# Rows of w_down gated with g2 beside the up projection and kept in DRAM, in a one-core diffusion block

## The chip, the core and the metric

The kernel runs on one core of one Trainium2 chip. The metric is the device time of one execution in microseconds (us). Three runs of the kernel before gave 1491.38, 1489.22 and 1489.94 us; the median is 1489.94 us. A core has a TensorE (PE, with its weight loads shown apart as PEld), a VectorE (DVE), a ScalarE (ACT), a GpSimd (POOL) and a SyncE (SP). Here SP issues every DMA, and each engine works through its own instructions in the order in which they were built.

## What is computed

One block of a diffusion transformer on 1024 tokens of width 1024: adaLN modulation, neighbourhood attention, output projection, and then a gated feed-forward part of width 2816 with a convolution over the tokens. The part that matters here is the last line:

```
def conv_ffn(h, w_up, conv_w, conv_b, w_down):
    a, g = jnp.split(h @ w_up, 2, axis=-1)
    return (a * jax.nn.gelu(dwconv_centred(g, conv_w, conv_b), approximate=False)) @ w_down

x = x + g2 * conv_ffn(modulate(rms_norm(x, p['norm2']), sh2, sc2), *p['ffn'])
```

`g2` is one row of 1024 numbers, the same for every token. Multiplying the result by `g2` is the same as multiplying every row of `w_down` by `g2` first, and this is what the kernel does, in both forms.

## The kernel before, in words

All matrix products are done with operands that are split into a rounded high part and a rest, so that each product is three matmuls (high x high, high x rest, rest x high). The high part is a copy on ACT, the rest a subtraction on DVE or POOL. Both projections of the feed-forward part use a Winograd form: seven products of half-size blocks in place of eight.

**Up projection** (L736 to L835). The 2816 columns come as 22 chunks of 128, taken in 11 blocks `i` of two chunks. A block has two parts, `part` 1 (the gate g) and `part` 0 (the value a), and each part has seven products `op`, in the order of `WORD`. That makes 154 steps; a step is 12 matmuls of 128x512. For each step `prep_up` (L678) makes the weight operand `u`: ACT copies the high part (L687), POOL subtracts the rest (L688). The operands live in 8 slots (tags `rh` and `rl`), so a new one can be made once PE has used an old one. DVE combines the seven products: `raw_up` (L673 to L675) and L686 form sums of weights, `put` (L757) adds PSUM banks and multiplies a by the gate, `conv` (L780) applies the token convolution, `finish` (L799) forms the sums for the down projection. SP stores them to `act_dram`.

**Down projection** (L837 to L931). The 11 blocks are taken in groups of 2, 3, 3 and 3, with seven products each. `load_raw` (L853) loads the two 128x1024 pieces of `w_down` of a block into tiles `dr` and multiplies them by `g2b`, the row g2 laid out on all 128 partitions: the piece `m` = 0 on POOL, the piece `m` = 1 on DVE. `prep_b` (L874) forms the Winograd sums of the pieces in place (L887 to L893) and splits them into `db` (L895 on ACT, L896 on DVE or POOL). `prep_a` (L865) loads the stored activations into `da` and splits them (L870 on ACT, L871 on DVE or POOL). `down_mm` (L899) multiplies, and DVE adds each bank onto the residual `acc` (L914).

What sets the order: the code is written as one stream, and a scheduler places each instruction on its engine's queue ahead of the run, earlier than written where it finds the engine free. The queues are then fixed. An instruction that waits holds everything behind it on its engine. The gate row `g2b` (L834) takes the slot of the first weight tile of the up projection, so it is there from the first few blocks on.

The lines that matter for the change:

```
SP.dma_start(out=r, in_=w_down[fc * P:(fc + 1) * P, :])
(DVE if m in DG else POOL).tensor_tensor(r, r, g2b, ALU.mult)
```

Of the kernel before, what the change touches and what calls it, by code (L numbers as in the profile page):

```python
# [10 lines left out]
F32 = mybir.dt.float32  # L11
F32R = mybir.dt.float32r
AF = mybir.ActivationFunctionType
ALU = mybir.AluOpType
# [4 lines left out]
P = 128  # L19
D = 1024  # L20
# [10 lines left out]
NF = DFF // P  # L31
# [5 lines left out]
HALF = 512  # L37
# [13 lines left out]
NA = ()  # L51
WD, SQD = range(8), ()
LAG = 1
DG = (1,)
HP_ = (3, 5, 6)
RL = 6
WORD = (1, 2, 5, 6, 7, 3, 4)
DORD = (2, 1, 5, 6, 3, 7, 4)

# [2 lines left out]
def block_kernel(ctx, tc, x, ctxt, cc, w_mod, b_col, b_row, n1, n2, w_qkv, gains, rpb_t, mask_i, mask_r, w_o,  # L62
                 w_up, conv_w, conv_b, w_down, comb, out):
    nc = tc.nc
    PE, ACT, DVE, POOL, SP = nc.tensor, nc.scalar, nc.vector, nc.gpsimd, nc.sync

    def pool(name, bufs=1, space=None, side=None):
        kw = {}
        if space is not None:
            kw["space"] = space  # L70
        if side is not None:
            kw["side"] = side
        if space is not DRAM:
            kw["reuse_waits"] = "tile"
        return tc.tile_pool(name=name, bufs=bufs, **kw)
# [8 lines left out]
    dram = ctx.enter_context(pool("dram", space=DRAM))  # L84
# [22 lines left out]
    o_dram = dram.tile([NPAIR, P, SEQ], F32, name="o_dram")  # L107
    g_dram = dram.tile([2, D], F32, name="g_dram")
    x1_dram = dram.tile([NB, P, D], F32, name="x1_dram")
    act_dram = dram.tile([NF // 2, P, 7, HALF], F32, name="act_dram")  # L110

    big = ctx.enter_context(pool("big", side="right"))
# [2 lines left out]
    def slot(tag, name, dt=F32R, shape=(P, D)):  # L115
        return big.tile(list(shape), dt, tag=tag, bufs=SLOTS[tag], name=name)
# [39 lines left out]
        DVE.tensor_scalar(ss, ss, 1.0 / D, EPS, ALU.mult, ALU.add)  # L156
        POOL.tensor_tensor(ss, ss, mhalf[:, 0:1], ALU.pow)

    # adaLN of the attention branch, normalised and modulated tokens, transposed and split
    att = ExitStack()  # L160
    sa = att.enter_context(pool("sa"))

# [106 lines left out]
            if si == 3:  # L269
                DVE.tensor_tensor(b1, pc[:, 1], bcol[:, 0:8].unsqueeze(2).broadcast_to([P, KC, 2]), ALU.add)  # L270

    # attention, with the projections of the next pair of heads in between
    sb = att.enter_context(pool("att"))
    mi = sb.tile([P, 3 * P], F32, name="mi")
    SP.dma_start(out=mi, in_=mask_i)
# [179 lines left out]
        DVE.tensor_tensor(res[a:b], po[a:b], tmp[a:b], ALU.add)  # L455
        SP.dma_start(out=o_dram[p, a:b, u * 2 * P:(u + 1) * 2 * P], in_=res[a:b])

    # adaLN of the rest, a little at a time
    def mod_gen():
        order = [2, 3, 4, 5]  # L460
        for sgi in order:
# [27 lines left out]
                        DVE.scalar_tensor_tensor(dst, dst, 1.0, n2c[:, nk * hf:nk * (hf + 1)], ALU.add, ALU.mult)  # L489
                yield  # L490

    # output projection: its first half runs beside the attention of the last heads
    xpool = ctx.enter_context(ExitStack())
    x1, wo, g1b, xsb = {}, [], [], []
    HP = NPAIR // 2
# [106 lines left out]
    filler(10 ** 6)  # L602
    att.close()

    # rest of the output projection, second norm, operands of the Winograd form (seven products of halves
    # in place of eight) of the up projection: A is w_up^T in 2 x 2 blocks, B the tokens in 2 x 2 blocks
    ff = ctx.enter_context(ExitStack())
    usb = ff.enter_context(pool("ffn"))
    BT = {}
    btags = ["bA"] * 12 + ["bB"] * 10 + ["wa"] * 6  # L610
    for i, op in enumerate(WORD):
        for j in range(4):
            tag = btags[4 * i + j]
# [3 lines left out]
            else:  # L617
                BT[op, hl, kk] = usb.tile([P, 2, HALF], F32R, tag=tag, bufs=12 if tag == "bA" else 10,
                                          name=f"b{op}{hl}{kk}")
# [26 lines left out]
            ACT.activation(h, r, AF.Copy)  # L646
            (POOL if op in HP_ else DVE).tensor_tensor(l, r, f(h), ALU.subtract)

    # up projection, gate with the token convolution; the gated rows and their sums go out for the down projection
    NP2 = NF // 2  # L650
    lo_, hi_ = slice(0, HALF), slice(HALF, SEQ)
    uraw, uop = {}, {}
    parts = [(i, part) for i in range(NP2) for part in (1, 0)]
    useq = [(0, 1, 1), (0, 1, 2), (0, 0, 1), (0, 0, 2)] + [(0, part, op) for part in (1, 0) for op in WORD[2:]]
    useq += [(i, part, op) for i, part in parts[2:] for op in WORD]
    cnt = [0]
# [21 lines left out]
    def prep_up(i, part, op):  # L678
        if (i, part) == (0, 1) and op in (1, 2):
            s = xslot(f"u{i}_{part}_{op}", F32R)  # L680
        else:
            s = slot(("rh", "rl")[cnt[0] % 2], f"u{i}_{part}_{op}", shape=(P, 2, HALF))
            cnt[0] += 1
        r = uraw[i, part]
        if op == 3:
            DVE.tensor_tensor(r[3], r[2], r[6], ALU.subtract)  # L686
        ACT.activation(s[:, 0], r[op], AF.Copy)  # L687
        POOL.tensor_tensor(s[:, 1], r[op], f(s[:, 0]), ALU.subtract)  # L688
        uop[i, part, op] = s
        if op == 4 and parts.index((i, part)) + 2 < len(parts):  # L690
            raw_up(*parts[parts.index((i, part)) + 2])
# [51 lines left out]
    def up_part(i, part, res):  # L743
# [23 lines left out]

        for op in WORD:
            bank = {1: x, 6: x, 2: z, 5: y, 3: y, 7: w, 4: w}[op]
# [10 lines left out]
    def conv(fc, g, y):  # L780
        ACT.activation(y, g, AF.Identity, bias=cb[:, fc:fc + 1], scale=cw[:, fc, 1:2])  # L781
        y8, g8 = (a.rearrange("p (m j) -> p m j", j=8) for a in (y, g))
        w0, w2 = cw[:, fc, 0:1], cw[:, fc, 2:3]
        R = ROWS

        def tap(o, i, w):
            DVE.scalar_tensor_tensor(o, i, w, o, ALU.mult, ALU.add)  # L787

        tap(y8[:, :, 1:], g8[:, :, :7], w0)
        tap(y8[:, R:, 0:1], g8[:, :-R, 7:8], w0)  # L790
        tap(y8[:, 1:R, 0:1], g8[:, (NB - 1) * R:NB * R - 1, 7:8], w0)
        tap(y8[:, :, :7], g8[:, :, 1:], w2)
        tap(y8[:, :-R, 7:8], g8[:, R:, 0:1], w2)
        tap(y8[:, (NB - 1) * R:NB * R - 1, 7:8], g8[:, 1:R, 0:1], w2)
        ACT.activation(y, y, AF.Gelu)
# [3 lines left out]
    def finish(i, y):  # L799
# [8 lines left out]
        SP.dma_start(out=act_dram[i, :, 3:5, :], in_=sa_)  # L808
        SP.dma_start(out=act_dram[i, :, 5:7, :], in_=sb_)

    sw = ps.tile([P, SEQ], F32, tag="s", bufs=1, name="sw")
    late_p1 = usb.tile([P, HALF], F32, name="late_p1")
    nprep, gens, g, y, late = 2, {}, {}, {}, []
    for k, (i, part, op) in enumerate(useq):
        while nprep < min(k + 1 + UA, len(useq)):
            prep_up(*useq[nprep])
            nprep += 1
        if (i, part) not in gens:
            if part:
                g[i] = [slot("wx", f"g{i}_{m}", F32) for m in range(2)]  # L820
                y[i] = [slot("t4", f"y{i}_{m}", F32) for m in range(2)]
            gens[i, part] = up_part(i, part, g[i] if part else y[i])
        next(gens[i, part])
        if op == WORD[-1]:
            if part:
                for m in range(2):
                    conv(2 * i + m, g[i][m], y[i][m])
                for o, p in late:
                    DVE.tensor_tensor(o, p, o, ALU.mult)
                late.clear()  # L830
            else:
                finish(i, y[i])
                if i == 0:
                    g2b = slot("gb", "g2b", F32)  # L834
                    SP.dma_start(out=g2b, in_=g_dram[1:2, :].broadcast_to([P, D]))  # L835

    # down projection, also in seven products; rows of w_down scaled by the gate g2  # L837
    xt = ps.tile([P, 2, HALF], F32, tag="s", bufs=1, name="dx")
    tr = [ps.tile([P, HALF], F32, tag="tr", bufs=3, name=f"dtr{j}") for j in range(3)]
    pq = [ps.tile([P, HALF], F32, tag="pq", bufs=2, name=f"dpq{j}") for j in range(2)]  # L840
# [12 lines left out]
    def load_raw(c):  # L853
        for m in range(2):
            if rt[0] % 14 < 8:
                r = xsb[0].tile([P, D], F32, tag="x1", bufs=NB, name=f"dr{c}_{m}")
            else:
                r = slot("wa", f"dr{c}_{m}", F32)
            rt[0] += 1
            fc = 2 * c + m  # L860
            SP.dma_start(out=r, in_=w_down[fc * P:(fc + 1) * P, :])
            (DVE if m in DG else POOL).tensor_tensor(r, r, g2b, ALU.mult)
            raws[c, m] = r

    def prep_a(q):  # L865
# [8 lines left out]
    def prep_b(q):  # L874
        n, op = seq[q]
        if q == 0:
            for c in groups[0]:
                load_raw(c)
        if op == RL and n + 1 < len(groups):
            for c in groups[n + 1]:  # L880
# [99 lines left out]
```

## Time and profile before

| | |
|---|---|
| median of three runs | 1489.94 us (1489.22 to 1491.38) |
| span of the profiled execution | 1491.8 us |
| mean granted TensorE clock | 0.974 |
| first POOL product of the up projection (L688) | starts at 788.1 us |
| first matmul of the down projection (L909) | starts at 1242.2 us |
| last matmuls of the down projection | 1487 us |

The profiled execution's span is 1.9 us longer than the median of the runs. How to read the rows below: a group of instructions is shown by line, engine, operation and tiles written and read, with its count and its mean or its least, median and greatest duration in nanoseconds. A window row gives the busy time of each engine in a stretch, with the number of instructions in brackets, the granted clock (PEclk), the share of the DMA engines in use and the rate. A row of waits gives who waited for whom, the total in us, the number of times and the longest. A duration in the records includes time in which an instruction was started but held up.

### The profile page before, as it was taken

The page shows a single profiled execution, that of the slowest core. Times are in us where ns is not written, and L with a number is a line of the kernel's source. Part 1 is how long each engine was busy: PE and PEld are TensorE (multiplying, and loading weights), DVE is VectorE, ACT ScalarE, POOL GpSimd, SP SyncE. Part 2 cuts the span into 40 slices and gives each one's busy share as a digit, 9 for nine tenths or more (in the row PEclk, how much of TensorE's full clock was granted, in tenths as well). Part 3 has the DMA queues.
Part 4 walks back from the last instruction along what each step waited for, and adds up shares of the span by engine and source line. Part 5 has one row for each costly group of instructions (what it writes and reads, how often), then busy time and mean ns, then how long its engine had stood idle before and what let it go on. Part 6 is the DMA issues. An engine that isn't in the chain of part 4 may idle for free.

```text
span 1491.8 us, 22077 instructions
## 1 busy us (share of the span) xinstructions
PE 1386.5 (93%) x7396; PEld 1200.0 (80%) x7396; DVE 1208.1 (81%) x2392; ACT 738.1 (49%) x1601; POOL 805.7 (54%) x672
## 2 busy tenths in 40 slices
PE   6689999999999999999996999999999987898998
PEld 2589889898989899888885777888888865686887
DVE  6778878888888878866589889788877779988884
ACT  6575645555565656645465434344343334244541
POOL 1455544545454546744368545555545568474872
PEclk9899999999999999999997999999999998899999
DMA  9612221313131202262132132233332347433343
GB/s 315 161 37 60 64 87 55 92 51 103 49 101 45 77 14 73 69 152 76 50 129 99 64 108 101 96 106 106 107 106 99 106 137 286 155 100 127 110 131 105
DMA packets 84827, 153.27 MB, mean 103 GB/s; under 512 B 9945, under 2 KB 49001, under 8 KB 84713
## 3 DMA queue, kind: packets, MB, share of 16 engines
q1 hardware_dynamic: 84712, 151.86, 32.7%
q8 instruction: 58, 0.95, 0.3%
q14 instruction: 57, 0.46, 0.1%
HBM read 119.05 MB, written 32.78 MB: 102 GB/s over the span
## 4 chain that ended last, share of the span: by engine, by line
PE 60%; DVE 20%; DMA 7%; POOL 5%; issue 4%; ACT 3%; SPq 0%; DVEq 0%; POOLq 0%; ACTq 0%
PE pg L740 8%; PE pa L740 7%; PE sw L740 6%; PE pq L301 5%; PE pq L303 5%; PE pq L305 5%; DMA mr<-in_w_mod_dram 2%; DVE y L787 2%; DVE p L410 2%; POOL u L688 2%; PE s L398 2%; PE po L448 2%; PE po L449 2%; PE py L525 2%; PE py L526 2%
## 5 line engine op out<-in xcount | busy, mean ns | idle before, releaser
L688 POOL TENSOR_TENSOR u<-ur,u 128x512 fp32r<-128x512 f32 x154 | 231.9, 1519 | 176.8 <-ACT u L687 175.1
L417 POOL TENSOR_TENSOR p<-p,m 128x640 f32<-128x640 f32 (+1 forms) x128 | 157.3, 1230 | 157.0 <-DVE m L413 116.0
L301 PE MATMUL pq<-wh,hth 128*128 128x384 f32 (+1 forms) x640 | 219.7, 343 | 17.1 <-DVE kn L340 15.3
L305 PE MATMUL pq<-wh,htl 128*128 128x384 f32 (+1 forms) x640 | 215.2, 336 | 2.4 <-DVE htl L194 1.4
L303 PE MATMUL pq<-wl,hth 128*128 128x384 f32 (+1 forms) x640 | 215.0, 336 | 0.5 <-POOL wl L147 0.5
L687 ACT ACTIVATE u<-ur 128x512 fp32r<-128x512 f32 x154 | 93.9, 628 | 116.1 <-PE sw L740 45.4
L412 ACT ACTIVATE p<-p,m 128x640 f32<-128x640 f32 (+1 forms) x128 | 102.9, 804 | 84.3 <-DVE m L410 75.2
L301 PEld LDWEIGHTS pq<-wh,hth 128*128 128x128 f32 x640 | 124.8, 195 | 23.1 <-DVE kn L340 9.2
L325 POOL TENSOR_TENSOR qss<-qss,mhalf 128x4 f32<-128x4 f32 (+1 forms) x80 | 79.9, 999 | 97.0 <-DVE qss L324 82.8
L305 PEld LDWEIGHTS pq<-wh,htl 128*128 128x128 f32 x640 | 124.7, 195 | 3.2 <-DVE htl L194 3.2
L303 PEld LDWEIGHTS pq<-wl,hth 128*128 128x128 f32 x640 | 124.8, 195 | 1.6 <-issue 0.9
L787 DVE SCALAR_TENSOR_TENSOR y<-g,cw,y 128x896 f32<-128x896 f32 (+1 forms) x132 | 102.8, 842 | 19.2 <-ACT y L781 19.1
L449 PE MATMUL po<-pt,v 128*128 128x256 f32 x352 | 93.3, 293 | 2.1 <-DVE pt L437 2.1
L448 PE MATMUL po<-pt,v 128*128 128x256 f32 x352 | 93.8, 289 | 0.1
L895 ACT ACTIVATE db<-dr 128x512 fp32r<-128x512 f32 x77 | 47.4, 629 | 87.3 <-PE dx L911 55.7
L871 POOL TENSOR_TENSOR da<-da 128x512 fp32r<-128x512 f32 x44 | 74.9, 1725 | 27.4 <-ACT da L870 27.4
L896 POOL TENSOR_TENSOR db<-dr,db 128x512 fp32r<-128x512 f32 x44 | 64.9, 1494 | 45.6 <-ACT db L895 34.3
L410 DVE CUSTOM_DVE_ANT_0 p<-s,bias 128x640 f32<-128x640 f32 x96 | 78.3, 816 | 9.5 <-PE s L399 8.9
L436 ACT ACTIVATE pt<-pl 128x384 fp32r<-128x384 f32 (+1 forms) x128 | 58.0, 461 | 47.6 <-PE pl L429 46.6
L471 DVE SCALAR_TENSOR_TENSOR macc<-mr,cs,macc 128x256 f32<-128x256 f32 x112 | 65.0, 581 | 13.9 <-DMA mr<-in_w_mod_dram 13.0
L437 DVE TENSOR_TENSOR pt<-pl,pt 128x384 fp32r<-128x384 f32 (+1 forms) x128 | 65.4, 516 | 6.7 <-ACT pt L436 6.2
L449 PEld LDWEIGHTS po<-pt,v 128*128 128x128 f32 x352 | 66.6, 189 | 4.0 <-DVE pt L437 3.4
(258 smaller groups left out, 4184.3 us busy)
## 6 DMA issues: line engine op xcount, KB each, us to landing
ur<-in_w_up_dram SPq DMA_DIRECT2D x44, 512.0 KB
da<-act_dram SPq DMA_DIRECT2D x77, 256.0 KB
mr<-in_w_mod_dram SPq DMA_DIRECT2D x128, 128.0 KB
dr<-in_w_down_dram SPq DMA_DIRECT2D x22, 512.0 KB
wraw<-in_w_qkv_dram SPq DMA_DIRECT2D x56, 192.0 KB
mraw<-in_w_mod_dram SPq DMA_DIRECT2D x16, 512.0 KB
act_dram<-sa SPq DMA_DIRECT2D x11, 512.0 KB
act_dram<-y SPq DMA_DIRECT2D x11, 512.0 KB
```

What stands on the lines that cost most here:

```text
L301: PE.matmul(pq[:, c0:], hth[t][:, k, :], wh[:, c0:], start=(k == 0), stop=False)
L303: PE.matmul(pq[:, c0:], hth[t][:, k, :], wl[:, c0:], start=False, stop=False)
L305: PE.matmul(pq[:, c0:], htl[t][:, k, :], wh[:, c0:], start=False, stop=(k == KC - 1))
L410: DVE.tensor_tensor_reduce(out=dst, in0=src, in1=bb, scale=1.0, scalar=3e38, op0=ALU.add, op1=ALU.min, accum_out=m[:, 0:1])
L412: ACT.activation(w[:, :n], w[:, :n], AF.Exp, bias=m[:, 0:1], scale=-1.0, accum_out=m[:, 1:2])
L417: POOL.tensor_tensor(w[:, :n], w[:, :n], m[:, 2:3].broadcast_to([P, n]), ALU.mult)
L448: PE.matmul(po, v, th[:, j].rearrange("p a b -> p (a b)"), start=(m == 0), stop=False)
L449: PE.matmul(po, v, tl[:, j].rearrange("p a b -> p (a b)"), start=False, stop=(m == len(blks) - 1))
L687: ACT.activation(s[:, 0], r[op], AF.Copy)
L688: POOL.tensor_tensor(s[:, 1], r[op], f(s[:, 0]), ALU.subtract)
L740: PE.matmul(bank, a, b, start=(start and k == 0 and n == 0), stop=(k == 3 and n == 2), skip_group_check=True)
L787: DVE.scalar_tensor_tensor(o, i, w, o, ALU.mult, ALU.add)
```

## The change

`load_raw` no longer multiplies. A new function `gate_w` loads a half row piece (128x512) of `w_down`, multiplies it by the matching half of `g2b` on POOL, in one of two buffers `wg`, and stores it to a new DRAM tensor `wg_dram`. It is called 44 times within the up projection, in the code at every third step from step 16 on. `load_raw` loads the pieces from `wg_dram`.

```diff
-DG = (1,)
+G0 = 16
...
+    wg_dram = dram.tile([NF, P, D], F32, name="wg_dram")
...
+    def gate_w(n):
+        fc, hf = divmod(n, 2)
+        c = slice(hf * HALF, (hf + 1) * HALF)
+        r = usb.tile([P, HALF], F32, tag="wg", bufs=2, name=f"wg{n}")
+        SP.dma_start(out=r, in_=w_down[fc * P:(fc + 1) * P, c])
+        POOL.tensor_tensor(r, r, g2b[:, c], ALU.mult)
+        SP.dma_start(out=wg_dram[fc, :, c], in_=r)
...
         next(gens[i, part])
+        if k >= G0 and (k - G0) % 3 == 0 and (k - G0) // 3 < 2 * NF:
+            gate_w((k - G0) // 3)
...
-            SP.dma_start(out=r, in_=w_down[fc * P:(fc + 1) * P, :])
-            (DVE if m in DG else POOL).tensor_tensor(r, r, g2b, ALU.mult)
+            SP.dma_start(out=r, in_=wg_dram[fc])
```

The scheduler does not leave the gate products at every third step. It places all 44 of them among the first 55 of POOL's subtractions that follow the arrival of `g2b`. POOL in the middle of that stretch, before, where `u2_1_5` is the operand of block 2, part 1, product 5, and `ur` the raw weights:

```order
L688 TENSOR_TENSOR u2_1_2_10895<-ur2_1_0_10707,u2_1_2_10895 128x512
L688 TENSOR_TENSOR u2_1_1_10878<-ur2_1_0_10707,u2_1_1_10878 128x512
L688 TENSOR_TENSOR u2_1_5_10911<-ur2_1_2_10711,u2_1_5_10911 128x512
L688 TENSOR_TENSOR u2_1_6_10927<-ur2_1_2_10711,u2_1_6_10927 128x512
L688 TENSOR_TENSOR u2_1_7_10945<-ur2_1_1_10709,u2_1_7_10945 128x512
```

The same place now, where `wg12` is the thirteenth gated half piece:

```order
L689 TENSOR_TENSOR u2_1_2_10908<-ur2_1_0_10708,u2_1_2_10908 128x512
L689 TENSOR_TENSOR u2_1_1_10887<-ur2_1_0_10708,u2_1_1_10887 128x512
L818 TENSOR_TENSOR wg12_11548<-wg12_11548,g2b_10703 128x512
L689 TENSOR_TENSOR u2_1_5_10924<-ur2_1_2_10712,u2_1_5_10924 128x512
L689 TENSOR_TENSOR u2_1_6_10940<-ur2_1_2_10712,u2_1_6_10940 128x512
L818 TENSOR_TENSOR wg13_11605<-wg13_11605,g2b_10703 128x512
L689 TENSOR_TENSOR u2_1_3_10979<-ur2_1_0_10708,u2_1_3_10979 128x512
L818 TENSOR_TENSOR wg14_11683<-wg14_11683,g2b_10703 128x512
L689 TENSOR_TENSOR u2_1_7_10962<-ur2_1_1_10710,u2_1_7_10962 128x512
```

Between the subtractions stand gate products, four for every five. SP's queue at the same place before, where `act_dram` takes the stores of block 0:

```order
L667 DMA ur2_1_0_10707<-in_w_up_dram 128x1024
L667 DMA ur2_1_1_10709<-in_w_up_dram 128x1024
L800 DMA act_dram_86<-y0_0_10421 128x512
L667 DMA ur2_0_0_10853<-in_w_up_dram 128x1024
L808 DMA act_dram_86<-sa0_10694 128x1024
```

The same place of SP's queue now:

```order
L668 DMA ur2_1_1_10710<-in_w_up_dram 128x1024
L817 DMA wg4_11039<-in_w_down_dram 128x512
L819 DMA wg_dram_86<-wg3_10958 128x512
L801 DMA act_dram_87<-y0_0_10422 128x512
L817 DMA wg5_11091<-in_w_down_dram 128x512
L819 DMA wg_dram_86<-wg4_11039 128x512
L817 DMA wg6_11145<-in_w_down_dram 128x512
L668 DMA ur2_0_0_10862<-in_w_up_dram 128x1024
L819 DMA wg_dram_86<-wg5_11091 128x512
L817 DMA wg7_11226<-in_w_down_dram 128x512
L819 DMA wg_dram_86<-wg6_11145 128x512
L809 DMA act_dram_87<-sa0_10695 128x1024
```

The store of a gated piece waits for POOL, and the loads of weights and the stores of activations now stand behind such stores; a load of a piece waits until the store out of its buffer has landed. The end of the up projection on POOL before, where `dr1_0` is the first piece of block 1 of `w_down`:

```order
L688 TENSOR_TENSOR u10_1_6_13215<-ur10_1_2_12999,u10_1_6_13215 128x512
L862 TENSOR_TENSOR dr1_0_13542<-dr1_0_13542,g2b_10702 128x1024
L688 TENSOR_TENSOR u10_1_7_13233<-ur10_1_1_12997,u10_1_7_13233 128x512
L688 TENSOR_TENSOR u10_1_3_13250<-ur10_1_0_12995,u10_1_3_13250 128x512
L688 TENSOR_TENSOR u10_1_4_13278<-ur10_1_1_12997,u10_1_4_13278 128x512
L688 TENSOR_TENSOR u10_0_2_13318<-ur10_0_0_13141,u10_0_2_13318 128x512
L862 TENSOR_TENSOR dr2_0_13644<-dr2_0_13644,g2b_10702 128x1024
L688 TENSOR_TENSOR u10_0_1_13302<-ur10_0_0_13141,u10_0_1_13302 128x512
```

The same place now:

```order
L689 TENSOR_TENSOR u10_1_6_13380<-ur10_1_2_13148,u10_1_6_13380 128x512
L689 TENSOR_TENSOR u10_1_7_13398<-ur10_1_1_13146,u10_1_7_13398 128x512
L689 TENSOR_TENSOR u10_1_3_13415<-ur10_1_0_13144,u10_1_3_13415 128x512
L689 TENSOR_TENSOR u10_1_4_13447<-ur10_1_1_13146,u10_1_4_13447 128x512
L689 TENSOR_TENSOR u10_0_2_13487<-ur10_0_0_13298,u10_0_2_13487 128x512
L689 TENSOR_TENSOR u10_0_1_13471<-ur10_0_0_13298,u10_0_1_13471 128x512
```

The gate products that stood between the subtractions, each waiting there for its piece to land, are gone. Apart from that, PE, DVE and ACT keep almost the order that they had.

## The prediction

> **What bounds the kernel now.** I read the totals of the page first, then busy times by stretch, then the waits of PE and POOL, then single instructions where PE stood still.
>
> ```profile
> PE 1386.5 (93%) x7396; PEld 1200.0 (80%) x7396; DVE 1208.1 (81%) x2392; ACT 738.1 (49%) x1601; POOL 805.7 (54%) x672
> ```
>
> PE is the bound overall, but 93% is an average. The stretches of the feed-forward part:
>
> ```profile
> core 0: us, PE busy (x) PEld busy (x) DVE busy (x) ACT busy (x) POOL busy (x), PEclk, DMA share, GB/s
> 833.00:991.00 158.00, 157.07 (x672) 125.63 (x672) 132.80 (x156) 64.21 (x96) 84.98 (x56) 1.00 0.31 104
> 991.00:1180.00 189.00, 189.00 (x814) 152.58 (x813) 154.81 (x187) 75.73 (x117) 97.54 (x68) 1.00 0.30 102
> 1180.00:1240.00 60.00, 54.39 (x231) 42.87 (x231) 48.81 (x54) 22.35 (x34) 35.17 (x20) 1.00 0.41 139
> 1240.00:1300.00 60.00, 46.90 (x171) 35.71 (x170) 58.13 (x61) 18.86 (x34) 44.52 (x21) 0.86 0.64 227
> ...
> 1345.00:1365.00 20.00, 14.45 (x54) 10.80 (x54) 16.14 (x22) 9.43 (x16) 11.87 (x7) 0.91 0.48 157
> 1365.00:1488.00 123.00, 122.21 (x540) 100.85 (x538) 89.72 (x111) 46.82 (x76) 71.13 (x48) 1.00 0.37 109
> ```
>
> From 991 to 1180 PE never waits: 814 matmuls in 189 us, 0.232 us each, so a step of 12 takes 2.79 us. At that price the 231 matmuls of 1180 to 1240 need 53.6 us, so 6.4 us are lost there; 171 need 39.7, so 20.3 are lost from 1240 to 1300; 54 need 12.5, so 7.5 are lost from 1345 to 1365. **34 us** are lost around the passage from the up to the down projection, and from 833 on little elsewhere (672 matmuls need 156 of the first 158). Part of the loss is clock: where PE had stood idle, PEclk falls (0.86, 0.91).
>
> Who held PE there:
>
> ```profile
> PE dx L909 <- DVE acc L914: 5.4, 2, 4.7
> PE dpq L909 <- DVE acc L914: 4.8, 2, 4.0
> PE dpq L909 <- DVE tmp L762: 4.3, 1, 4.3
> PE pg L740 <- ACT tmp L772: 3.2, 1, 3.2
> PE dtr L909 <- ACT db L895: 2.6, 1, 2.6
> PE sw L740 <- DVE g L760: 1.5, 1, 1.5
> ```
>
> Mostly DVE, which is 97% busy in that window. Why DVE is so slow there is the point on which this case turns. Single instructions of POOL and of DVE, and least/median/greatest durations in ns of four groups:
>
> ```profile
> 1251.78 5.15 POOL L871 TENSOR_TENSOR da<-da 128x512 fp32r<-128x512 f32 x3
> ...
> 1253.99 1.77 DVE L889 TENSOR_TENSOR dr<-dr,dr 128x512 f32<-128x512 f32 x1
> 1255.69 1.78 DVE L893 TENSOR_TENSOR dr<-dr,dr 128x512 f32<-128x512 f32 x1
> 1257.39 1.79 DVE L766 TENSOR_TENSOR y<-tmp,y 128x512 f32<-128x512 f32 x1
> ...
> L766 DVE TENSOR_TENSOR y<-tmp,y x43: 672/705/2824, 854.1 to 1271.4; 128x512 f32<-128x512 f32 x43
> L774 DVE TENSOR_TENSOR tmp<-sw,tmp x22: 676/680/694, 829.1 to 1248.1; 128x512 f32<-128x512 f32 x22
> L688 POOL TENSOR_TENSOR u<-ur,u x154: 1254/1446/3130, 788.1 to 1232.6; 128x512 fp32r<-128x512 f32 x154
> L787 DVE SCALAR_TENSOR_TENSOR y<-g,cw,y x132: 226/1133/2195, 837.4 to 1242.3; 128x896 f32<-128x896 f32 x44, 128x112 f32<-128x112 f32 x44, 128x15 f32<-128x15 f32 x44
> ```
>
> L774 has one input in PSUM and takes 0.68 us every time. L766, the same size with both inputs in SBUF, takes 0.67 when free and up to 2.82. When both engines have work, DVE starts such an instruction every 1.70 us and POOL takes 5.15/3 = 1.72: they take turns. POOL alone needs 1.25, so a DVE instruction with two SBUF inputs occupies what the two share for 0.45. I call this the **turn**; POOL's products and DVE's two-SBUF-input products compete for it, PSUM-fed ones do not.
>
> **What goes.** 11 products on POOL and 11 on DVE of 128x1024:
>
> ```profile
> L862 POOL TENSOR_TENSOR dr<-dr,g2b x11: 2347/2417/2857, 1182.2 to 1354.1; 128x1024 f32<-128x1024 f32 x11
> L862 DVE TENSOR_TENSOR dr<-dr,g2b x11: 1208/1214/3408, 1192.0 to 1363.5; 128x1024 f32<-128x1024 f32 x11
> ...
> POOL dr L862 <- DMA dr<-in_w_down_dram: 13.5, 4, 5.3
> ```
>
> From 1180 to 1300 POOL also stood 13.5 us waiting for pieces to land, with subtractions queued behind. The clearest case is three of these products in a row:
>
> ```profile
> 1265.30 8.34 POOL L862 TENSOR_TENSOR dr<-dr,g2b 128x1024 f32<-128x1024 f32 x3
> ...
> 1268.58 2.85 DVE L806 TENSOR_TENSOR sb<-y 128x512 f32<-128x512 f32 x1
> 1271.36 2.82 DVE L766 TENSOR_TENSOR y<-tmp,y 128x512 f32<-128x512 f32 x1
> ...
> 1274.84 0.80 PE L909 MATMUL dpq<-db,da 128*128 128x512 f32 x1 [4.02 <-DVE acc L914]
> 1275.43 0.63 PE L910 MATMUL dpq<-db,da 128*128 128x512 f32 x1
> 1275.86 0.63 PE L911 MATMUL dpq<-db,da 128*128 128x512 f32 x1
> ...
> 1275.00:1280.00 5.00, 4.90 (x11) 3.44 (x12) 5.00 (x8) 1.26 (x2) 0.00 (x0) 0.50 0.98 349
> ```
>
> DVE's instructions each wait for one of POOL's, PE waits 4.02 us for DVE, and afterwards its matmuls start 0.43 us apart at a PEclk of 0.50: 11 in 5 us, another 2.45 us lost. With the products gone, 6.5 us of the 20.3 go. Of the other 13.8, the waits stand behind the `da` and `db` subtractions, which stay; the turn loses some 18 us of gate work in those 60 us (five products of 2.4 and five of 1.2), and I give it 6. From 1180 to 1240 POOL's waits for pieces and its four products delay the last operands `u` and DVE's sums: 5 of 6.4. From 1345 to 1365 the chain of work runs over a landing, then a product on POOL, then DVE:
>
> ```profile
> 1350.27 3.63 DMA dr<-in_w_down_dram
> ...
> 1354.07 2.36 POOL dr L862
> ```
>
> The 2.36 goes, the landing stays: 2.5 of 7.5. **Gain 20 us**, with 10 (only what is directly on the path) and 34 (all of it) as ends. Next in line is the subtraction work of `da` and `db`. The 22 loads stay, from another place in DRAM.
>
> **What comes.** 44 products of 128x512 on POOL, each half of the median of L862 on POOL (2.42): 1.21, together 53 us. They stand among 55 subtractions, which are 55 steps of PE, 153 us. POOL's own time has room: 85 busy in the 158 us from 833 on, and 138 with them. The turn has not. In a block of 14 steps (39 us) it carries 14 subtractions at 1.25 (17.5), 18 DVE products of 512 at 0.45 (6 of L673 to L675, 2 of L686, 2 of two-SBUF `put`, 4 of L766, 4 of `finish`: 8.1) and 12 of L787, priced by their length (3.6, an estimate): 29.2 us, 75%. The gates add 44/55 x 14 = 11.2 products, 13.6 us: 42.8 of 39. Over 55/14 = 3.93 blocks that is 168 us in place of 153: **15 us** even if the turn is never idle. It will be idle at times. The nearest stretch with gates beside the up projection is 1180 to 1240: four products on POOL and three on DVE, 13.3 us, cost 6.4 us of PE, 0.48 for each us; 53 us would cost **25.5**. From 1240 to 1300 the rate is 20.3 for 18, which would make 59, but there the first operands of the down projection are made as well. Below, the least is nothing, if gates fall only where nobody wants the turn. I take 25, from the nearest row, with 0 and 59 as ends.
>
> The Trainium skill (SBUF — State Buffer, "Who interferes with whom") says that a VectorE instruction with two SBUF inputs and a GpSimd instruction that reads SBUF exclude each other for the whole instruction, and that one-SBUF-input instructions do not contend. The rows of L766 and L774 agree with who contends. By whole instructions at 0.68 and 1.25 us the block would need 48.7 us, and the stretch would be 38 us longer, not 15; the measured 1.70 for a pair, under 0.68 + 1.25, speaks for the smaller price.
>
> **The queues.** 88 more DMAs are issued by SP, and each store waits for POOL with loads of weights and stores of activations behind it. The nearest prices:
>
> ```profile
> 1342.02 3.82 DMA da<-act_dram
> ...
> 1245.18 4.11 DMA act_dram<-y
> ```
>
> A load of 256 KB landed after 3.82 us and a store after 4.11, both beside other traffic. A buffer then takes 3.82 + 1.25 + 4.11 = 9.2 us, and two buffers give a product every 4.6, against the 153/44 = 3.5 that the order leaves. If a load and a store together stay under 5.7 us, the chain is hidden; the DMA share in the stretch is 0.31, and I count it at nothing, with 50 us as the other end (44 x 4.6 = 202 against 153). The rate of the added 23 MB over 158 us is 146 GB/s beside the 104 of the row, below what 1240 to 1300 moved (227).
>
> **Sum.** 1491.8 + 25 - 20 = 1496.8 for a profiled execution. Its span is 1.9 above the median of the runs, so 1495. A difference of 0.2% (3 us) is about the least that can be told from no change.
>
> **Rivals.**
> - *The gates fit.* POOL idles 73 us of the 158, and PE lost nothing with the turn 75% in use; if the products fall into gaps, the loss is 0 to 8 and the gain stands: 1489.9 - 20 + 4 = 1474. Against it: 110% of the turn. Chance 0.30.
> - *The piece chain decides* (slower). Where load and store of a piece exceed 5.7 us, POOL waits at a gate with the next `u` behind it, and PE behind that: up to 50 lost, 20 won, 1520. For it: the store stands in SP's queue behind waits on DVE. Against: the low DMA share. Chance 0.10.
> - *The gain is smaller.* The `da` and `db` subtractions take over the passage, and only the 8 to 10 us directly on the path are won: 1507. Chance 0.12.
> - That the products are not moved at all, or twice, is excluded by POOL's order. Chance 0.
>
> The forecast has 0.48, by itself from 1484 to 1508. All of the first rival and a tenth of the forecast lie over 0.2% below 1489.9: faster 0.34. Within 0.2%: 0.16. Slower: 0.50. The range leaves out a third of the first rival below and most of the second above: 1471 to 1514.
>
> **What would show it.** In the profile after, from 833 us on: POOL near 90% busy until the last gate product; the mean of L688 near 1.7 us (1.5 if the gates fit); DVE close to 100%; fewer than 650 matmuls in the first 158 us; the last gate product after 1010 us (near 990 if they fit). POOL waits on the landing of `wg` by more than 20 us would show the second rival. In the passage: the 4.02 us wait gone, and the sum of idle and half-clock time near 14 us in place of 34. The forecast is wrong if PE stays at 100% up to 1000 us, or if the passage keeps more than 25 us of loss.

## The result and the profile after

The changed kernel took 1503.3 us (median of 4 runs, 1497.4 to 1507.6); the kernel before took 1489.6 beside it. The ratio is 1.0096, 95% interval 1.0068 to 1.0124; measured once more, 1.0085 (1.0070 to 1.0100). It is slower, by some 13 us. The profiled execution took 1503.0 us, with a span of 1501.2. That is only 9.4 more than the span before, 1491.8, which lay above the median of its runs.

The stretches of the changed kernel, as in the prediction, and 833 to 1040 as one. Lines have shifted by one in the up projection's functions (L688 is now L689), and by 11 or 12 in the down projection.

```profile
core 0: us, PE busy (x) PEld busy (x) DVE busy (x) ACT busy (x) POOL busy (x), PEclk, DMA share, GB/s
833.00:991.00 158.00, 135.64 (x541) 106.56 (x539) 132.96 (x129) 52.33 (x77) 116.99 (x79) 0.93 0.57 191
991.00:1180.00 189.00, 183.18 (x769) 146.95 (x770) 150.93 (x175) 70.97 (x111) 107.42 (x74) 0.98 0.36 126
833.00:1040.00 207.00, 178.82 (x711) 140.45 (x710) 175.59 (x172) 70.15 (x105) 152.64 (x102) 0.93 0.56 188
1180.00:1240.00 60.00, 60.00 (x259) 48.46 (x258) 48.42 (x62) 26.21 (x40) 32.60 (x23) 1.00 0.26 92
1240.00:1300.00 60.00, 55.16 (x226) 43.30 (x226) 49.88 (x59) 23.70 (x39) 29.16 (x19) 0.94 0.66 237
1345.00:1365.00 20.00, 19.94 (x89) 16.16 (x88) 14.08 (x21) 9.60 (x16) 14.42 (x11) 1.00 0.48 171
```

The kernel before, from 833 to 1040:

```profile
833.00:1040.00 207.00, 206.07 (x882) 165.16 (x882) 176.47 (x208) 86.67 (x130) 110.49 (x73) 1.00 0.30 102
```

At 0.232 us a matmul the passage has lost 0, 7.6 and 0 us in its three stretches, where it lost 34 before. (It comes 30 us later now, with the first matmul of the down projection at 1272.7 us, but still within these stretches; 1300 to 1345, not among the rows, loses nothing either, with 198 matmuls in 45 us.) But between 833 and 1040 us 711 matmuls stand for 165 us of 207: **42 us are lost** in a stretch that lost 2 before. 28 of them are idle (207 - 178.8). In the other 14 the matmuls themselves took longer (178.8 - 165); the PEclk of 0.93 accounts for some 12 of these (165/0.93 - 165, an estimate). So most of the passage's loss went, and a larger one came in the up projection.

The gated pieces there: the gate products and who held them (least/median/greatest ns; first and last start).

```profile
L818 POOL TENSOR_TENSOR wg<-wg,g2b x44: 1261/1299/2190, 830.0 to 1025.6; 128x512 f32<-128x512 f32 x44
L819 SPq DMA_DIRECT2D wg_dram<-wg x44: 319/327/1283, 831.3 to 1026.9; - x44
its engine sat idle before it (us, times) until:
  DMA wg<-in_w_down_dram: 39.7, 22
```

44 products take from 830.0 to 1025.6 us, one every 4.55. POOL stands 39.7 us in front of a product whose piece has not landed, with the subtractions `u` behind it; for ACT it waits only 5.0 us in this time. So 55 subtractions take 195.6 us, one every 3.56, where a step of PE takes 2.79. A piece of the chain of waits of this kernel (start, us, what):

```profile
943.05 3.58 DMA wg<-in_w_down_dram
...
946.79 1.28 POOL wg L818
...
948.09 2.96 DMA wg_dram<-wg
...
951.06 3.54 DMA wg<-in_w_down_dram
...
954.76 1.30 POOL wg L818
...
956.08 2.01 DMA wg_dram<-wg
...
958.15 3.32 DMA wg<-in_w_down_dram
```

Load, product, store, load, in one buffer, without a gap: a round of 8.0 us (943.05 to 951.06), for two buffers 4.0 us a product. PE itself mostly waited for ACT and DVE:

```profile
PE pa L741 <- ACT tmp L773: 12.6, 3, 5.0
PE sw L741 <- DVE tmp L775: 4.8, 1, 4.8
PE pg L741 <- POOL u L689: 4.4, 1, 4.4
```

### The profile page after: what moved, and what is told of

Same layout as the page of the kernel before. It is cut to its first block, busy times and chain, and to the rows that moved or that the text cites. A ratio compares the mean times of both kernels' runs of the same rounds, so it can differ in the third digit from the quotient of the medians.

```text
span 1501.2 us, 22266 instructions
## 1 busy us (share of the span) xinstructions
PE 1387.2 (92%) x7396; PEld 1200.8 (80%) x7396; DVE 1205.3 (80%) x2381; ACT 739.5 (49%) x1601; POOL 830.8 (55%) x705
## 3 DMA queue, kind: packets, MB, share of 16 engines
q1 hardware_dynamic: 97384, 174.94, 36.5%
## 4 chain that ended last, share of the span: by engine, by line
PE 59%; DVE 19%; DMA 9%; POOL 5%; issue 4%; ACT 4%; SPq 1%; DVEq 0%; POOLq 0%; ACTq 0%
PE pg L741 6%; PE pa L741 6%; PE pq L302 5%; PE pq L304 5%; PE pq L306 5%; PE sw L741 4%; DVE y L788 3%; POOL u L689 2%; DMA wg<-in_w_down_dram 2%; PE dtr L920 2%; PE dtr L921 2%; PE dtr L922 2%; PE po L449 2%; PE s L399 2%; PE po L450 2%
## 5 line engine op out<-in xcount | busy, mean ns | idle before, releaser
L689 POOL TENSOR_TENSOR u<-ur,u 128x512 fp32r<-128x512 f32 x154 | 230.8, 1510 | 123.8 <-ACT u L688 118.6
L302 PE MATMUL pq<-wh,hth 128*128 128x384 f32 (+1 forms) x640 | 218.6, 342 | 15.9 <-DVE kn L341 14.2
L688 ACT ACTIVATE u<-ur 128x512 fp32r<-128x512 f32 x154 | 93.5, 628 | 128.3 <-PE sw L741 48.2
L788 DVE SCALAR_TENSOR_TENSOR y<-g,cw,y 128x896 f32<-128x896 f32 (+1 forms) x132 | 122.0, 984 | 20.8 <-ACT y L782 20.8
L818 POOL TENSOR_TENSOR wg<-wg,g2b 128x512 f32<-128x512 f32 x44 | 64.7, 1472 | 43.7 <-DMA wg<-in_w_down_dram 39.7
L882 POOL TENSOR_TENSOR da<-da 128x512 fp32r<-128x512 f32 x44 | 67.8, 1565 | 26.4 <-ACT da L881 26.3
```

Of the source, the lines that this page charges most:

```text
L302: PE.matmul(pq[:, c0:], hth[t][:, k, :], wh[:, c0:], start=(k == 0), stop=False)
```

## The experiments

Two causes were to be told apart: the turn between POOL and DVE (TURN), and the buffer round that holds POOL (CHAIN, HOLD). All runs in one table. The cost is the ratio's distance to that of the kernel without any gate, times 1491 us. "DVE's work" is the busy time of the same 380 DVE instructions of the up projection from 800 us on (L674 to L676, L687, L763, L767, L775, L788, L805 to L808, and the form of L761 that reads `tmp` alone). "Waits" is POOL's time in front of a piece that had not landed. By the intervals of the two ratios, a cost is uncertain by some 3 to 5 us.

| kernel | median us | ratio to before (95%) | cost us | matmuls 833 to 1040 | DVE's work us | waits us |
|---|---|---|---|---|---|---|
| before | 1489.6 | 1 | | 882 | 344.2 | |
| changed | 1503.3 | 1.0096 (1.0068, 1.0124) | 36.5 | 711 | 362.9 | 39.7 |
| changed, again | 1504.5 | 1.0085 (1.0070, 1.0100) | 34.9 | 706 | 359.2 | 39.0 |
| no gate | 1467.6 | 0.9851 (0.9837, 0.9866) | 0 | 884 | 333.6 | |
| products only | 1491.7 | 1.0005 (0.9994, 1.0017) | 23.0 | 779 | 360.5 | |
| memsets in place of products | 1463.4 | 0.9834 (0.9810, 0.9859) | -2.5 | 880 | 332.8 | |
| products on DVE | 1486.4 | 0.9972 (0.9956, 0.9988) | 18.0 | 801 | 368.4 with them | |
| transfers only | 1472.0 | 0.9862 (0.9842, 0.9883) | 1.6 | 866 | 335.7 | |
| memsets and transfers | 1489.6 | 0.9985 (0.9970, 1.0000) | 20.0 | 772 | 322.0 | 53.9 |
| three buffers | 1506.4 | 1.0112 (1.0095, 1.0129) | 38.9 | 705 | 363.3 | 15.8 |
| three buffers, loads on ACT | 1505.5 | 1.0105 (1.0080, 1.0130) | 37.9 | 703 | 365.8 | 26.4 |
| spread | 1498.3 | 1.0050 (1.0030, 1.0069) | 29.7 | 813 | 372.4 | 15.7 |
| spread, three buffers | 1503.1 | 1.0059 (1.0040, 1.0077) | 31.0 | 819 | 368.6 | 30.0 |
| gate at the end | 1468.9 | 0.9846 (0.9829, 0.9864) | -0.7 | 881 | 337.6 | |

### The gain alone

```diff
-            gate_w((k - G0) // 3)
+            pass
...
-            SP.dma_start(out=r, in_=wg_dram[fc])
+            SP.dma_start(out=r, in_=w_down[fc * P:(fc + 1) * P, :])
```

> Left out: the gate altogether, no pieces and no products, neither beside the up projection nor in the down projection, which loads w_down itself. Gives the gain alone. If all 41 us that the changed kernel loses between 833 and 1040 us come from the pieces, and the passage keeps the 7.6 us of loss that it has in the changed kernel: 1503 - 41 + 2 = 1464 us, 1460 to 1468. If a part of the gain or the loss is the placing of the rest (other order, other queues), above 1470 us. Both CHAIN and TURN expect the first.

```profile
833.00:1040.00 207.00, 206.15 (x884) 165.26 (x883) 176.97 (x208) 87.21 (x130) 110.26 (x74) 1.00 0.30 102
...
1180.00:1240.00 60.00, 56.53 (x240) 45.03 (x239) 45.87 (x58) 29.72 (x47) 28.82 (x21) 0.98 0.55 195
1240.00:1300.00 60.00, 59.23 (x249) 47.56 (x248) 54.42 (x76) 19.96 (x34) 26.12 (x18) 0.96 0.54 193
```

884 matmuls as before the change, and a passage that loses 6.6 us (489 matmuls x 0.232 = 113.4 of 120). All that the products cost before was 0.0149 x 1491 = **22 us** (20 to 24 by the interval). The spans of the two profiles differ by more, 27.8 us (1491.8 and 1464.0): the profiled execution before was slower than its median, the one without gate faster (1466.2 against 1467.6). And all that the changed kernel loses beside the up projection comes from the pieces.

### The products alone

```diff
-        SP.dma_start(out=r, in_=w_down[fc * P:(fc + 1) * P, c])
-        POOL.tensor_tensor(r, r, g2b[:, c], ALU.mult)
-        SP.dma_start(out=wg_dram[fc, :, c], in_=r)
+        POOL.tensor_tensor(wgs[n % 2], g2b[:, c], g2b[:, c], ALU.mult)
```

> Left out: the gate in the result. The 44 loads and 44 stores of pieces go; POOL still makes 44 products of 128x512 (g2b with itself, into two scratch tiles), which stand among 49 subtractions in place of 55; the down projection loads w_down itself. Theory TURN: the loss of the up projection stays, 15 us at perfect packing and 25 to 45 as it went; with the gain of the passage kept, 1476 to 1505 us, and the mean of L689's subtraction is 1.6 us or more. Theory CHAIN: POOL has nothing to wait for, the loss falls under 10 us: 1462 to 1472 us.

The products take from 832.1 to 960.1 us. By the trace they stand among 38 subtractions, not 49, so they are denser than in the changed kernel (55).

```profile
833.00:1040.00 207.00, 186.47 (x779) 147.38 (x778) 180.98 (x184) 75.73 (x113) 159.11 (x110) 0.98 0.27 94
```

Without a single transfer 23 us remain of 36. CHAIN as the sole cause falls. PE's idle time (20.5 us) is spent in front of DVE and of ACT, and only 1.2 us in front of an operand `u`:

```profile
PE sw L741 <- DVE tmp L763: 9.7, 2, 5.8
PE pa L741 <- ACT tmp L773: 6.6, 2, 3.5
PE pa L741 <- POOL u L689: 1.2, 1, 1.2
```

The largest group of DVE, the convolution L788, without gate and then with the products (busy us, mean ns):

```profile
L788 DVE SCALAR_TENSOR_TENSOR y<-g,cw,y 128x896 f32<-128x896 f32 (+1 forms) x132 | 100.7, 829 | 20.9 <-ACT y L782 20.9
```

```profile
L788 DVE SCALAR_TENSOR_TENSOR y<-g,cw,y 128x896 f32<-128x896 f32 (+1 forms) x132 | 114.6, 930 | 22.7 <-ACT y L782 22.7
```

The same instructions take longer. Over all 380, DVE's work grows from 333.6 to 360.5 us: 0.61 us for each product, and the kernel takes 23 us longer. The product here, which reads one tile twice, is a little lighter than in the changed kernel (mean 1315 ns against 1472).

### The same time on POOL without reads

The product-only kernel, with POOL as busy, but with instructions that only write:

```diff
-        POOL.tensor_tensor(wgs[n % 2], g2b[:, c], g2b[:, c], ALU.mult)
+        if n == 0:
+            POOL.tensor_tensor(wgs[:, c], g2b[:, c], g2b[:, c], ALU.mult)
+            return
+        POOL.memset(wgs, 0.0)
+        POOL.memset(wgs[:, 0:256], 0.0)
```

> The product-only kernel (1491.7 us, no transfers, gate missing from the result) with each product but the first replaced by two memsets of 128x1024 and 128x256 on POOL, which take about as long (estimate from the 128x128 memset's 0.2 us: about 1.2 us together) and read nothing. Theory TURN (a product costs because it and the two-SBUF instructions of DVE hold each other up: DVE's instructions of the up projection take 360.5 us in all in the product-only kernel and 333.6 without gate): the cost goes although POOL is as busy: 1466 to 1474 us, DVE's total back to 330 to 340. Theory LATE U (a product costs because the subtractions u stand behind it on POOL): the cost stays, 1486 to 1494 us.

```profile
833.00:1040.00 207.00, 205.18 (x880) 164.95 (x879) 175.09 (x210) 84.92 (x128) 159.44 (x159) 1.00 0.30 100
```

```profile
L819 POOL MEMSET wgs<- 128x1024 f32 x43 | 41.1, 956 | 1.4
L820 POOL MEMSET wgs<- 128x256 f32 x43 | 13.5, 314 | 1.3
```

POOL is busy for 159.4 us of the 207, as in the product-only kernel (159.1), the subtractions `u` stand behind 1.27 us of memsets each time, and nothing is lost: 880 matmuls, DVE's work 332.8. So a product is not dear because it takes POOL's time or delays `u`, but because it **reads** SBUF beside DVE's instructions with two SBUF inputs. The Trainium skill (SBUF — State Buffer, "Who interferes with whom") says that such DVE instructions contend with a GpSimd instruction that reads SBUF, not with one that only writes it; the two runs agree, 23.0 us against nothing (-2.5, within the uncertainty). It says of instructions with one SBUF input that they do not contend outside DVE's two-port modes, a condition that the prediction leaves out and that no run here shows.

### The products on DVE

```diff
-        POOL.tensor_tensor(wgs[n % 2], g2b[:, c], g2b[:, c], ALU.mult)
+        DVE.tensor_tensor(wgs[n % 2], g2b[:, c], g2b[:, c], ALU.mult)
```

> The product-only kernel (1491.7 us, no transfers, gate missing from the result) with the 44 products of 128x512 on DVE in place of POOL, 0.6 us each when free, 27 us in all. Theory TURN, in the form that DVE's time is what PE waits for: as dear as on POOL, since there each product lengthened DVE's work by 0.61 us (26.9 us over 44): 1486 to 1496 us. Theory LATE U: POOL is free of gates, 1467 to 1475 us.

```profile
L816 DVE TENSOR_TENSOR wgs<-g2b 128x512 f32<-128x512 f32 x44 | 37.2, 880 | 0.6 <-DMA g2b<-g_dram 0.6
```

No transfer, no gate on POOL, and still 18 us. DVE's work grows by 34.8 us (331.2 for the 380 and 37.2 for the products, 0.88 each and not 0.6), and the kernel takes about half of that longer. LATE U falls, and the range of TURN just holds. But here DVE is simply full: the 44 products start from 833.9 to 913.8 us, and from 833 to 914 DVE is busy 79.6 of 81 us and 19 us of PE are lost. Without gate DVE was 85% busy from 833 to 1040 us (177 of 207). So this run prices DVE's time and is no second proof of the turn.

### The transfers

The change without its products:

```diff
-        POOL.tensor_tensor(r, r, g2b[:, c], ALU.mult)
```

> Left out: the product, so the gate is missing from the result. The 44 pieces are loaded and stored again ungated, and the down projection loads the stored copy; POOL has no gate work. The runs so far: no gate at all 1467.6 us, products without transfers 1491.7, both 1503.3. If the transfers cost by themselves (SP's queue, the other loads and stores), the 11.6 us between the last two are found again: 1474 to 1481 us. If they cost only by holding POOL at a product, with the subtractions u behind it, nothing is left: 1465 to 1471 us.

1.6 us by the ratio, within the uncertainty of nothing; the median, 1472.0 us, falls between the two ranges. But this kernel's pieces wait for neither `g2b` nor POOL and are through by 894 us, so it shows what 88 transfers cost, not what they cost at the pace of the changed kernel. For that, POOL must wait for each piece without the turn:

```diff
-        POOL.tensor_tensor(r, r, g2b[:, c], ALU.mult)
+        if n < 2:
+            POOL.tensor_tensor(r, r, g2b[:, c], ALU.mult)
+        else:
+            POOL.memset(r, 0.0)
+            POOL.memset(r, 0.0)
```

> The changed kernel with all 88 transfers and two buffers, and each product but the first two replaced by two memsets of the piece on POOL (about 0.5 us each), which read nothing; the rows of w_down come out as zeros, so the down projection's part of the result is left out. POOL still waits for each piece to land (WAW) with the subtractions u behind it, but nothing is shared with DVE's reads. The changed kernel costs 11.6 us more than its products alone, the transfers alone 4.4. Theory HOLD (POOL standing for a piece costs by itself): 1478 to 1485 us. Theory TOGETHER (the wait costs only because DVE and POOL, held up by each other, have no time to make it good): 1468 to 1475 us.

```profile
833.00:1040.00 207.00, 187.04 (x772) 146.80 (x771) 146.97 (x183) 74.82 (x112) 137.42 (x151) 0.98 0.62 202
```

```profile
L821 POOL MEMSET wg<- 128x512 f32 x42 | 22.1, 526 | 58.5 <-DMA wg<-in_w_down_dram 53.9 <-issue 4.5
L822 POOL MEMSET wg<- 128x512 f32 x42 | 21.6, 526 | 0.9
```

```profile
DVE ur L687 <- POOL u L689: 30.3, 7, 9.8
DVE ur L674 <- POOL u L689: 8.5, 6, 2.4
```

20 us are lost again, 1489.6 us where HOLD had expected at most 1485, and this time DVE's work is shorter than without gate (322.0 us). It stands idle instead: 39 us behind POOL's late subtractions, whose inputs it has to overwrite; before the change the same two lines waited 9 us there. And PE stands in front of POOL directly, 13.4 of its 20 idle us:

```profile
PE pa L741 <- POOL u L689: 10.8, 3, 5.7
PE pg L741 <- POOL u L689: 2.6, 2, 2.4
```

POOL has little to spare: while it handles the pieces it waits 53.9 us for them and 1.5 us for ACT, and its 57 subtractions take from 833.6 to 1018.7 us, one every 3.25 where a step of PE takes 2.79. So pieces that are moved at POOL's pace cost by themselves, and TOGETHER falls. The run doesn't part POOL's standing from SP's queue: ACT stands 14.2 us for the landing of stores of sums here, 5.4 without gate. The pieces are about as dense as in the changed kernel (57 subtractions and 55), and the last one is through at about the same time (1018 us).

### More buffers, and a wider spread

A third buffer, from a tile that is idle by then:

```diff
-        r = usb.tile([P, HALF], F32, tag="wg", bufs=2, name=f"wg{n}")
+        r = usb.tile([P, HALF], F32, tag="wg", bufs=3, name=f"wg{n}")
...
-    late_p1 = usb.tile([P, HALF], F32, name="late_p1")
+    late_p1 = usb.tile([P, HALF], F32, tag="wg", bufs=3, name="late_p1")
```

> The gate pieces get a third buffer: the tile late_p1, idle by then, goes into the same rotation. Everything else is as in the changed kernel. Theory CHAIN (POOL stands for the load, product, store, load of a buffer, and the subtractions u behind it wait too): in the changed kernel POOL waits 39.7 us on the landing of wg and 41 us of PE are lost between 833 and about 1040 us; three buffers divide the round of 9 us by three, so the waits on wg fall below 15 us, the loss to 20 to 28 us, and the time from 1503 to 1483 to 1492 us. Theory TURN (POOL's products and the two-SBUF-input instructions of DVE hold each other up): the same products meet the same DVE work, a little more densely, so the waits on wg may fall, but the loss stays at 38 to 45 us and the time at 1500 to 1507 us.

```profile
L818 POOL TENSOR_TENSOR wg<-wg,g2b x44: 1257/1436/2239, 831.6 to 997.0; 128x512 f32<-128x512 f32 x44
...
  DMA wg<-in_w_down_dram: 15.8, 9
```

```profile
ACT g L773 <- DMA act_dram<-sa: 15.4, 3, 8.0
```

The round is faster (a product every 3.85 us) and POOL's waits for pieces fall to 15.8 us, but nothing is won. CHAIN expected 1483 to 1492, and this misses it; TURN's 1500 to 1507 holds. The trace shows another wait, which the products alone did not have: ACT stands for the landing of stores of sums, which share SP's queue with the pieces (9.7 us in the changed kernel, 5.4 before). So SP was relieved of the loads:

```diff
-        SP.dma_start(out=r, in_=w_down[fc * P:(fc + 1) * P, c])
+        ACT.dma_start(out=r, in_=w_down[fc * P:(fc + 1) * P, c])
```

> The kernel with three buffers, nothing left out, in which ACT's queue and not SP's issues the loads of the pieces. With three buffers POOL waited only 15.8 us for pieces in place of 39.7, yet the time stayed at 1506.4 us. There SP stood 46.8 us in front of a piece's load until an earlier store had landed, with the stores of sums behind it, whose landing ACT's g waits for (ACT's waits on the landing of sa: 15.4 us, and none in the product-only kernel). Theory QUEUE (this standing in SP's queue is what the third buffer leaves): 1490 to 1498 us, ACT's waits on sa gone. Theory DENSER (the third buffer only lets the products follow closer on each other, and DVE's work stays as long): 1501 to 1509 us. If ACT itself stands for the stores by more than 30 us, the run tells neither.

```profile
ACT u L688 <- DMA wg_dram<-wg: 23.7, 7, 5.8
ACT tmp L773 <- DMA wg_dram<-wg: 14.5, 2, 9.2
```

ACT's waits on the sums are all but gone (1.1 us), but it stands 38 us for the stores of pieces. By its own condition this run tells neither theory. What exactly keeps the three-buffer kernel 16 us above the products alone stays open.

Then the pieces were held back to their steps, with two buffers and with three:

```diff
+PACE = 3
...
-    def gate_w(n):
+    def gate_w(n, s):
...
+        ACT.activation(r[:, 0:1], f(s[:, 0, 0:1]), AF.Copy)
         SP.dma_start(out=r, in_=w_down[fc * P:(fc + 1) * P, c])
...
-            gate_w((k - G0) // 3)
+            gate_w((k - G0) // 3, uop[useq[min(k + PACE, len(useq) - 1)]])
```

> The 44 pieces are spread over the up projection: before each load ACT copies one column of a low-numbered operand u of that step into the piece, which holds the load back to that step, so that the products stand among some 132 subtractions in place of 55. Two buffers, as in the changed kernel. CHAIN: a piece every 8.4 us against a round of 4.6 per piece: hidden, the waits on wg fall below 10 us, the loss below 8 us, the time is 1465 to 1473 us. TURN: 29.2 + 5.6 of 39 us per block: fits too, about the same time, 1465 to 1478. Theory TRAFFIC (the 88 transfers cost SP's queue and the other loads the same wherever they stand): 1490 us or more.

> The spread of the pieces and the third buffer in one kernel, nothing left out. The spread with two buffers took 1498.3 us; DVE's up projection work in it takes 372.4 us, 38.8 more than without gate, and POOL still waits 13.3 us for pieces. Theory DVE TIME (what counts is by how much the products lengthen DVE's work, wherever they stand): 1494 to 1501 us. Theory WAITS (the pieces' waits are what is left): 1485 to 1492 us.

The spread kernel by stretches:

```profile
833.00:1040.00 207.00, 194.43 (x813) 153.72 (x812) 173.71 (x189) 80.38 (x138) 134.06 (x88) 0.98 0.44 148
1040.00:1180.00 140.00, 135.07 (x575) 107.01 (x574) 118.02 (x130) 55.84 (x96) 96.42 (x64) 1.00 0.45 152
1180.00:1240.00 60.00, 56.21 (x233) 44.42 (x233) 49.42 (x53) 22.90 (x41) 41.05 (x28) 0.97 0.46 157
1240.00:1300.00 60.00, 52.84 (x206) 41.88 (x205) 50.30 (x67) 23.04 (x37) 24.09 (x16) 0.89 0.71 256
```

CHAIN and TURN expected the spread to fit (1465 to 1478). It costs 30 us with either number of buffers, and the loss has spread with the pieces: 18, 7, 6 and 12 us in the four stretches (each one's length less 0.232 a matmul), where the kernel without gate loses 2, 0, 4 and 2. DVE's work is even longer than in the changed kernel, by 35 to 39 us over that without gate, and PE's waits in the spread kernel name DVE and ACT and never an operand `u`. So the products lengthen DVE's work whether they stand dense or not. That all of the 30 us is theirs isn't shown: TRAFFIC's 1490 or more was met as well, POOL still waited 15.7 and 30.0 us for pieces, and no spread kernel without transfers was run. Of the ranges for three buffers neither holds by the median (1503.1 us); by the ratio (1.0059 x 1491 = 1500) DVE TIME's does.

### Again, and another place for the gate

> The changed kernel once more, beside the runs above on one chip: 1499 to 1507 us, a ratio of 1.006 to 1.011 to the kernel before, if the first measurement stands; its distance to the products alone (ratio 1.0005) is then 8 to 15 us.

It repeats the first measurement (table). The runs say that products of this kind are dear beside the up projection, on POOL as on DVE, and that they should go where DVE has time. At the end of the down projection it has. So the accumulators no longer start from x1, and gate and residual come last; `gate_w` goes, and `load_raw` loads `w_down` itself:

```diff
+            if n == 0 and op in (2, 5, 6, 4):
+                ACT.activation(d, o, AF.Copy)
+                continue
             DVE.tensor_tensor(d, o, d, ALU.add)
             if last and op in (1, 3, 7, 4):
+                DVE.tensor_tensor(d, d, g2b[:, col * HALF:(col + 1) * HALF], ALU.mult)
+                DVE.tensor_tensor(d, d, x1l[t][:, col * HALF:(col + 1) * HALF], ALU.add)
                 SP.dma_start(out=ov[t, :, :, col * HALF:(col + 1) * HALF], in_=d)
...
-        SP.dma_start(out=a_, in_=x1_dram[t])
...
+                SP.dma_start(out=r, in_=x1_dram[t])
+                x1l.append(r)
```

> A version with nothing left out and without any product of w_down: the accumulators begin with ACT's copy of the first sums in place of x1; after the last sum of each 128x512 block DVE multiplies it by g2 and adds x1, which is loaded when the last group begins. 32 more DVE instructions in the last 34 us, where DVE stands idle 1.35 us between two sums of PE (0.69 busy each); two of 0.6 us fit in there, and 1.2 us come behind the last sum. Against the kernel without any gate (1467.6 us): 1468 to 1473 us. If the passage from up to down needs the old start of the accumulators, or the last blocks are held up, 1475 us or more.

Its last DVE instructions:

```profile
1460.15 0.69 DVE L917 TENSOR_TENSOR acc<-dx,acc 128x512 f32<-128x512 f32 x1
1460.76 0.68 DVE L920 TENSOR_TENSOR acc<-acc,xl 128x512 f32<-128x512 f32 x1
1461.36 0.69 DVE L919 TENSOR_TENSOR acc<-acc,g2b 128x512 f32<-128x512 f32 x1
1462.08 0.69 DVE L920 TENSOR_TENSOR acc<-acc,xl 128x512 f32<-128x512 f32 x1
```

1468.9 us, 1.5% below the kernel before (0.9829 to 0.9864) and as fast, within the intervals, as with no gate at all. Behind DVE's sum of PE's last result (L917) stand one residual of the block before (L920), the last product and the last residual, some 2 us.

## Why the prediction was nearly right, and which step was wrong

**Direction and forecast.** Slower was forecast (1495, range 1471 to 1514; the forecast by itself 1484 to 1508), and 1503.3 came. By terms, from the table: gain 22 us where 20 was predicted, products 23 where 25 was predicted for the turn, and 12 to 14 for the pieces' transfers where nothing was counted. 1489.6 - 22 + 23 + 13 = 1504.

**The gain.** Right in size and place. The passage lost 7.6 us in place of the predicted 14, and the 4.02 us wait is gone.

**The turn.** Who contends was right, and 25 us is near the 23 of the product-only kernel. The price was in part luck: 0.48 us of PE for each us of gate work was read from 1180 to 1240, where POOL also stood 13.5 us for pieces; 23.0 for 53 us is 0.43. The account by packing beside it stands halfway. In the changed kernel its marks were missed: POOL was 74% busy (117 of 158; mark 90%), DVE 84% (133 of 158; mark 100%), the subtraction's mean 1.56 us (mark 1.7). But POOL stood for pieces there. In the product-only kernel, from 833 to 961 us, POOL was 91% busy and the subtraction's mean 1.70, with DVE at 90%; and by the prediction's own terms 44 products among 38 subtractions would need 38 x 29.2/14 + 53 = 132 us where PE needs 106, so 26 lost, and 23 were. Against the account stands the spread kernel, with 34.8 of 39 us in use: it should have lost nothing and lost 30, its transfers and waits for pieces included. So the packing is a fair estimate where the products stand dense, and seems too low where they don't; why isn't shown.

The mark of a last gate product after 1010 us was met (1025.6), but not by the turn, since without transfers the last one started at 960.1. The rival in which the gates fit, with 0 to 8 us lost, falls with the 23.

**The queues: the step that failed.** "A buffer then takes 3.82 + 1.25 + 4.11 = 9.2 us, and two buffers give a product every 4.6, against the 153/44 = 3.5 that the order leaves" stood there, and behind it "I count it at nothing", for the low DMA share. The product came every 4.55 us. (So close an agreement is luck too: the rounds shown take 7 to 8 us, and half of the products found their piece landed.) The chain of two buffers is a latency, three waits after each other, and a share of 0.31 or 0.57 of busy DMA engines says nothing of it. The mark set for the second rival, more than 20 us of POOL waiting on the landing of `wg`, was met with 39.7. By itself such pieces cost 20 us, with POOL behind PE's pace; with the products beside them they add 12 to 14. The rival had the mechanism, but with 50 us, and without the turn: its 1520 was too much.

**What stays open.** The products alone and the memsets with transfers cost 23 and 20 us, both together 35 to 36. The difference may lie in the density: the product-only kernel has 44 products among 38 subtractions, the changed one among 55. By packing, 55 would cost 15 and not 23, and the pieces would then cost 20 to 22. How their cost divides between POOL's standing and SP's queue wasn't settled; the third buffer took most of the first away, and the time did not fall. Nor is it shown how the standing reaches PE in the changed kernel, where PE names POOL's `u` for only 5.3 of its 28 idle us.

## What to carry to other kernels

Work for an idle engine isn't free because that engine is idle: ask what it reads together with the engine on which the bound one waits, and take the price from the nearest stretch where both ran, not from the idle engine's free time. When a load, an instruction and a store turn round in a few buffers, compare the round divided by the buffers with the pace that the order asks for, and count what is missing; the DMA share doesn't answer that. And before moving a product to another engine or stage, look whether linearity lets it move to the result, where there may be fewer and later ones: 16 blocks here in place of 44 pieces.

## What the runs showed of the hardware

- Writing alone on POOL didn't disturb DVE: 54.6 us of memsets (0.956 us for 128x1024, 0.314 for 128x256) left DVE's work at 332.8 us against 333.6, while 57.4 us of products made it 360.5.
- Two holds that cost 23 and 20 us alone cost 35 to 36 us together, not 43 (each uncertain by 3 to 5 us, and at another density).
- About a third of the loss was in slower matmuls: with PE idle 28 us in ten waits of 0.3 to 5.0 us between 833 and 1040 us, PEclk was 0.93, and the matmuls themselves took 14 us longer. In the product-only kernel, with 20.5 us idle, PEclk was 0.98 and they took 6 us longer (186.5 - 779 x 0.232).
